# A matrix product with bias and tanh: every engine's order fixed by hand, and an opening in two groups of row tiles and two parts of k

## The chip, the cores and the metric

The kernel runs on one core of one Trainium2 chip. The metric is the device time of one execution in microseconds; a lower time is better. The times shown are three runs of the kernel before, and one further run was executed with the hardware profiler.

## The reference

`a` is 4096 x 4096, `b` is 4096 x 4096, `bias` has 4096 elements, all in fp32. What must be computed:

```python
def reference(a, b, bias):
    return np.tanh(np.matmul(a, b) + bias)
```

## The kernel before

The product is made of matmuls of 128 x 128 weights (a piece of `a`, transposed, in fp16) and a moving operand of 128 x 512 (a piece of `b`, in fp16). There are 32 row tiles of 128 rows of `a`, 32 pieces of k of 128 each, and 8 column halves of 512, so 8192 matmuls. The columns are worked through in 4 chunks of 1024 (`NCW`). For one chunk all of `b`'s 4096 x 1024 piece lies in SBUF in eight tiles `b_0` to `b_7` of four pieces of k each, in two buffers: the next chunk is loaded while this one is worked on.

All loads are issued by POOL and convert fp32 to fp16 on the way. A tile is loaded by four DMAs, one for each quarter of the partitions (32 partitions each), because k is split over the partitions as four quarters of 1024. `load_b` (L55) loads 256 KB (in fp16) a DMA, `load_a` (L62) a quarter of the natural tile `an`. VectorE (DVE) then turns each 32 x 32 block of `an` into the tile `at` (`transpose_a`, L69), which is what the matmuls read as weights. When a PSUM bank has its 32 pieces of k, `finish` adds the bias on DVE (L90, `o_sb<-ps,bias_bc`), takes tanh on ScalarE (ACT, L96), and stores 256 KB from the SyncE queue (L99). `o_sb` has four buffers, `an` two, `at` four, PSUM eight banks.

The opening (matmuls of L131) works on four row tiles at once (`M0`), in eight slices of four pieces of k: it loads 128 KB of `a` four times and 256 KB of `b` four times for a slice, turns `a`, and lets 32 matmuls run into eight banks. After the eighth slice the eight banks are finished. The main loop (matmuls of L166) then goes through the other row tiles of chunk 0 and all row tiles of chunks 1 to 3, each with two banks of 32 matmuls. `load_row_tile` loads and turns the row tile two ahead, and two DMAs of the next chunk's `b` are issued with each row tile until its 32 are done.

The order in which each engine gets its instructions is not that of the text: Tile's scheduler plans it when the program is built. The program's text says what depends on what; the scheduler decides, for instance, whether DVE gets the turning of a later row tile before or after the bias add of the present one. Each engine then works strictly in the order that it was given.

Of the kernel before, what the change touches and what calls it, by code (L numbers as in the profile page):

```python
# [1 line left out]

# [5 lines left out]

P = 128
Q = 4
QP = 32
NB = 512
fp32 = mybir.dt.float32
fp16 = mybir.dt.float16


@with_exitstack
def kernel(
    ctx: ExitStack,
    tc: tile.TileContext,
    a: bass.AP,
    b: bass.AP,
    bias: bass.AP,
    out: bass.AP,
):  # L30
    nc = tc.nc
    M, K = a.shape
    K2, N = b.shape
    assert (M, K, K2, N) == (4096, 4096, 4096, 4096)

    KQ = K // Q
    KT = K // P
    MT = M // P
    NCW = 1024
    NC = N // NCW  # L40
    J = NCW // NB
    TB = 4
    M0 = 4
    SL = [4] * 8

    bpool = ctx.enter_context(tc.tile_pool(name="bpool", bufs=2))
    anat = ctx.enter_context(tc.tile_pool(name="anat", bufs=2))
    atp = ctx.enter_context(tc.tile_pool(name="atp", bufs=4))
    biasp = ctx.enter_context(tc.tile_pool(name="biasp", bufs=2))
    opool = ctx.enter_context(tc.tile_pool(name="opool", bufs=4))  # L50
    psum = ctx.enter_context(tc.tile_pool(name="psum", bufs=8, space=bass.MemoryType.PSUM))

    def load_b(dst, n0, t0, nt, q):
        src = b[ds(q * KQ + t0 * QP, nt * QP), ds(n0, NCW)]
        nc.gpsimd.dma_start(  # L55
            out=dst[ds(q * QP, QP), :, :],
            in_=src.rearrange("(t p) n -> p t n", p=QP),
        )

    def load_a(dst, m0, nmb, k0, kk, q):  # L60
        src = a[ds(m0, nmb * QP), ds(q * KQ + k0, kk)]
        nc.gpsimd.dma_start(  # L62
            out=dst[ds(q * QP, QP), :, :],
            in_=src.rearrange("(mb p) k -> p mb k", p=QP),
        )

    def transpose_a(at, an, mb0, nmb, nt):

        nc.vector.transpose(  # L69
            at[:, :, ds(mb0 * QP, nmb * QP)].rearrange("P t (mb p) -> P mb t p", p=QP),  # L70
            an[:, ds(mb0, nmb), :].rearrange("P mb (t k) -> P mb t k", k=QP),
        )

    def new_b(n0):
        return [bpool.tile([P, TB, NCW], fp16, name=f"b_{i}") for i in range(KT // TB)]

    def load_bias(n0):
        bias_bc = biasp.tile([P, NCW], fp32, name="bias_bc")
        src = bias[ds(n0, NCW)]
        nc.gpsimd.dma_start(  # L80
            out=bias_bc,
            in_=bass.AP(tensor=src.tensor, offset=src.offset, ap=[[0, P], *src.ap]),
        )
        return bias_bc

    def finish(ps, bias_bc, mi, n0, j, pieces=1):
        w = NB // pieces
        o_sb = opool.tile([P, NB], fp32, name="o_sb")
        for i in range(pieces):
            nc.vector.tensor_tensor(  # L90
                out=o_sb[:, ds(i * w, w)],
                in0=ps[:, ds(i * w, w)],
                in1=bias_bc[:, ds(j * NB + i * w, w)],
                op=mybir.AluOpType.add,
            )
            nc.scalar.activation(  # L96
                o_sb[:, ds(i * w, w)], o_sb[:, ds(i * w, w)], mybir.ActivationFunctionType.Tanh
            )
            nc.sync.dma_start(  # L99
                out=out[ds(mi * P, P), ds(n0 + j * NB + i * w, w)], in_=o_sb[:, ds(i * w, w)]  # L100
            )

    def load_row_tile(mi):
        an = anat.tile([P, Q, KQ], fp16, name="an")
        for q in range(Q):
            load_a(an, mi * P, Q, 0, KQ, q)
        at = atp.tile([P, KT, P], fp16, name="at")
        transpose_a(at, an, 0, Q, KT)
        return at


    b_cur = new_b(0)
    ps0 = [[psum.tile([P, NB], fp32, name="ps") for j in range(J)] for m in range(M0)]
    at0 = []
    t0 = 0
    for s, nt in enumerate(SL):
        an = anat.tile([P, M0 * Q, nt * QP], fp16, name="an")
        at = atp.tile([P, nt, M0 * P], fp16, name="at0", bufs=3)
        for q in range(Q):
            load_a(an, 0, M0 * Q, t0 * QP, nt * QP, q)  # L120
        for q in range(Q):
            load_b(b_cur[s], 0, t0, nt, q)
        for m in range(M0):
            transpose_a(at, an, m * Q, Q, nt)
        order = (
            [(t, m, j) for t in range(nt) for m in range(M0) for j in range(J)]
            if s < len(SL) - 1
            else [(t, m, j) for m in range(M0) for j in range(J) for t in range(nt)]
        )
        for t, m, j in order:  # L130
            nc.tensor.matmul(  # L131
                ps0[m][j],
                at[:, t, ts(m, P)],
                b_cur[s][:, t, ts(j, NB)],
                start=t0 + t == 0,
                stop=t0 + t == KT - 1,
            )
        t0 += nt

    bias_bc = load_bias(0)  # L140
    at_q = [load_row_tile(M0), load_row_tile(M0 + 1)]
    for m in range(M0):
        for j in range(J):
            finish(ps0[m][j], bias_bc, m, 0, j)


    todo = [(c, mi) for c in range(NC) for mi in range(MT) if (c, mi) >= (0, M0)]
    b_next, left = None, []
    for i, (c, mi) in enumerate(todo):
        if mi == 0:  # L150
            b_cur, bias_bc = b_next, bias_next
        if c + 1 < NC and mi == (M0 if c == 0 else 0):
            b_next = new_b(c + 1)
            left = [(s, q) for s in range(KT // TB) for q in range(Q)]
        if i + 2 < len(todo):
            at_q.append(load_row_tile(todo[i + 2][1]))
        for s, q in left[:2]:
            load_b(b_next[s], (c + 1) * NCW, s * TB, TB, q)
        left = left[2:]
        if c + 1 < NC and mi == MT - 4:  # L160
            bias_next = load_bias((c + 1) * NCW)
        at = at_q.pop(0)
        for j in range(J):
            ps = psum.tile([P, NB], fp32, name="ps")
            for t in range(KT):
                nc.tensor.matmul(  # L166
                    ps,
                    at[:, t, :],
                    b_cur[t // TB][:, t % TB, ts(j, NB)],
                    start=t == 0,  # L170
                    stop=t == KT - 1,
                )
            last = i == len(todo) - 1 and j == J - 1
            finish(ps, bias_bc, mi, c * NCW, j, pieces=4 if last else 1)


# [1 line left out]
_INS = ['a', 'b', 'bias']  # L178
_OUTS = [((4096, 4096), 'float32')]


# [23 lines left out]
```

## Time and profile before

| what | value |
|---|---|
| median of three runs | 1944.84 us (1944.42 to 1945.73) |
| the profiled execution's own time | 1943.61 us |
| its span, first to last instruction | 1941.8 us |
| mean granted TensorE clock | 0.973 of full |
| PE busy | 1812.3 us (93%), 8192 matmuls |
| DVE busy | 736.3 us (38%), 415 instructions |
| ACT busy | 162.6 us (8%) |
| POOL busy | 357.5 us (18%), 664 instructions |
| DMA over the span | 238.27 MB counted as fp16 or fp32 where it lands, mean 123 GB/s |

Busy time of an engine is the time in which it executes; what stands between busy stretches is waiting. The span is PE's busy time, the waits of PE, the time before its first matmul and the time after its last. A matmul of 512 columns at half clock takes twice as long and counts as busy, so a loss of clock hides in the busy time. In the rows, times are microseconds from the start of the span; a row that ends in `[5.19 <-DVE at L69]` says that the engine stood idle for 5.19 us before this work and that a DVE instruction of line 69, which writes `at`, ended the wait.

### The profile page before, as it was taken

The numbers are of one execution on the slowest core, as the hardware profiler recorded it, in microseconds if no ns is written. First come the engines' busy times: TensorE is split into PE (matmuls) and PEld (weight loads), VectorE is DVE, ScalarE is ACT, GpSimd is POOL, SyncE is SP. The second block draws the span as 40 slices with busy tenths as digits, with TensorE's granted clock in tenths as the row PEclk, the third lists the DMA queues.
The fourth block names the chain that finished last, engine by engine and source line by source line (L and its number), as shares of the span: only waits on it lengthen the run. The fifth ranks groups of instructions, "written<-read, shape, count | busy, mean of one in ns | idle before, by whom it ended". The sixth has DMA issues, their size and how long they took to land. (4 is left out here: it accounts for less than half of the span.)

```text
span 1941.8 us, 19313 instructions
## 1 busy us (share of the span) xinstructions
PE 1812.3 (93%) x8192; PEld 809.6 (42%) x8192; DVE 736.3 (38%) x415; ACT 162.6 (8%) x260; POOL 357.5 (18%) x664
## 2 busy tenths in 40 slices
PE   6698878799999888799999988889999999999998
PEld 2243333344444333344444433334444444444444
DVE  2433233344433333444443333334444444343431
ACT  0100000000000000000000000000000000000000
POOL 5411111011211111111121112111111111111100
PEclk9899989999999999899999999989999999999999
DMA  9976656466675566356667656556666655555531
GB/s 179 201 146 130 130 110 124 98 120 135 126 156 114 120 125 130 80 119 126 136 123 155 135 111 127 119 104 117 125 134 125 125 111 117 112 116 115 114 82 38
DMA packets 144710, 238.27 MB, mean 123 GB/s; under 512 B 31088, under 2 KB 31600, under 8 KB 144624
## 3 DMA queue, kind: packets, MB, share of 16 engines
q0 software_dynamic: 107328, 169.91, 52.4%
q1 hardware_dynamic: 37296, 67.13, 9.4%
q8 instruction: 64, 1.05, 0.2%
q14 instruction: 22, 0.18, 0.0%
HBM read 337.64 MB, written 67.11 MB: 208 GB/s over the span
## 5 line engine op out<-in xcount | busy, mean ns | idle before, releaser
L166 PE MATMUL ps<-b,at 128*128 128x512 f16 x7936 | 1753.2, 385 | 106.3 <-DVE at L69 106.3
L166 PEld LDWEIGHTS <-at 128*128 128x128 f16 x7936 | 784.3, 99 | 1075.1 <-DVE at L69 115.6
L90 DVE TENSOR_TENSOR o_sb<-ps,bias_bc 128x512 f32<-128x512 f32 (+1 forms) x259 | 177.0, 685 | 1154.0 <-PE ps L166 808.2
L69 DVE STREAM_TRANSPOSE at<-an 128x4096 f16<-128x4096 f16 (+1 forms) x156 | 569.3, 3663 | 47.5 <-DMA an<-in_a_dram 47.5
L62 POOL DMA_DIRECT2D an<-in_a_dram x528 | 286.4, 549 | 1455.0 <-DVE at L69 1433.5
L96 ACT ACTIVATE o_sb<-o_sb 128x512 f32<-128x512 f32 (+1 forms) x259 | 161.4, 624 | 1774.8 <-DVE o_sb L90 1774.8
L55 POOL DMA_DIRECT2D b<-in_b_dram x128 | 69.1, 544 | 48.6 <-PE ps L166 23.3
L131 PE MATMUL ps<-b,at 128*128 128x512 f16 x256 | 59.1, 392 | 18.3 <-DMA b<-in_b_dram 18.3
L131 PEld LDWEIGHTS <-at 128*128 128x128 f16 x256 | 25.3, 100 | 51.6 <-issue 24.5
L80 POOL DMA_DIRECT2D bias_bc<-in_bias_dram x4 | 2.2, 560 | 0.2 <-issue 0.2
L96 ACT ACT_TABLE_LOAD x1 | 1.3, 1283 | 0.7 <-PEq L189 0.7
L189 POOL MEMSET const-float32-0.0<- 128x1 f32 x1 | 0.1, 98 | 0.2 <-issue 0.2
L189 POOL MEMSET const-bfloat16-1.0<- 128x1 bf16 x1 | 0.1, 102 | 0.0
L189 POOL MEMSET const-float32-1.0<- 128x1 f32 x1 | 0.1, 98 | 0.0
L189 POOL MEMSET const-uint8-127<- 128x1 uint8 x1 | 0.1, 98 | 0.0
## 6 DMA issues: line engine op xcount, KB each, us to landing
an<-in_a_dram POOLq DMA_DIRECT2D x496, 256.0 KB, 5.3
out_dram<-o_sb SPq DMA_DIRECT2D x255, 256.0 KB, 2.3
b<-in_b_dram POOLq DMA_DIRECT2D x128, 256.0 KB, 7.9
an<-in_a_dram POOLq DMA_DIRECT2D x32, 128.0 KB, 7.5
bias_bc<-in_bias_dram POOLq DMA_DIRECT2D x4, 512.0 KB, 8.1
out_dram<-o_sb SPq DMA_DIRECT2D x4, 64.0 KB, 1.6
```

The source lines that it names most:

```text
L55: nc.gpsimd.dma_start(out=dst[ds(q * QP, QP), :, :], in_=src.rearrange("(t p) n -> p t n", p=QP),)
L62: nc.gpsimd.dma_start(out=dst[ds(q * QP, QP), :, :], in_=src.rearrange("(mb p) k -> p mb k", p=QP),)
L69: nc.vector.transpose(at[:, :, ds(mb0 * QP, nmb * QP)].rearrange("P t (mb p) -> P mb t p", p=QP), an[:, ds(mb0, nmb), :].rearrange("P mb ( ...
L80: nc.gpsimd.dma_start(out=bias_bc, in_=bass.AP(tensor=src.tensor, offset=src.offset, ap=[[0, P], *src.ap]),)
L90: nc.vector.tensor_tensor(out=o_sb[:, ds(i * w, w)], in0=ps[:, ds(i * w, w)], in1=bias_bc[:, ds(j * NB + i * w, w)], op=mybir.AluOpType.add,)
L96: nc.scalar.activation(o_sb[:, ds(i * w, w)], o_sb[:, ds(i * w, w)], mybir.ActivationFunctionType.Tanh)
L131: nc.tensor.matmul(ps0[m][j], at[:, t, ts(m, P)], b_cur[s][:, t, ts(j, NB)], start=t0 + t == 0, stop=t0 + t == KT - 1,)
L166: nc.tensor.matmul(ps, at[:, t, :], b_cur[t // TB][:, t % TB, ts(j, NB)], start=t == 0, stop=t == KT - 1,)
L189: nc = _bacc.Bacc("TRN2", target_bir_lowering=False, num_devices=1)
```

## The change

Tile's scheduler is switched off with `tc.manual_schedule()`: each engine gets its instructions in the order of the program's text. The main loop is written so that the load of a row tile stands three row tiles ahead (`ahead = 3`, with three `an` buffers), and its turning (`new_at`) two ahead, at the start of an iteration, before the matmuls and the bias adds of that iteration.

The opening works on eight row tiles instead of four, in two groups of four (`G`), and on k in two parts: the first eight pieces (`KS`), then the other 24. First part: group 0 goes through slices of 2, 2 and 4 pieces (`S0`), all eight banks at once, then group 1 (row tiles 4 to 7) does its eight pieces bank by bank. Each bank's sum of the first part gets the bias added and is put aside in SBUF in fp32 (`put_aside`, 16 adds of 128 x 512). Second part: group 0 goes through six slices of four pieces (`S2`), and `end` adds the sum put aside in place of the bias, followed by tanh and store; then group 1 does its 24 pieces bank by bank with its own `turn` of 128 x 3072 for each row tile. The sums put aside and group 1's `at` tiles lie in the second buffers of `b_0` to `b_7`, which chunk 1 needs only later. Group 1's first part is loaded by two loads of two row tiles each (four DMAs of 128 KB each), its second part by four loads of a row tile each (four DMAs of 192 KB each).

The diff (`...` stands for the removed lines of the old opening, which the kernel above shows):

```diff
--- before.py
+++ after.py
@@ -40,39 +40,49 @@
     NC = N // NCW
     J = NCW // NB
     TB = 4
-    M0 = 4
-    SL = [4] * 8
+    G = 4
+    KS = 8
+    S0 = [2, 2, 4]
+    S2 = [4] * 6
 
     bpool = ctx.enter_context(tc.tile_pool(name="bpool", bufs=2))
-    anat = ctx.enter_context(tc.tile_pool(name="anat", bufs=2))
+    anat = ctx.enter_context(tc.tile_pool(name="anat", bufs=3))
     atp = ctx.enter_context(tc.tile_pool(name="atp", bufs=4))
     biasp = ctx.enter_context(tc.tile_pool(name="biasp", bufs=2))
     opool = ctx.enter_context(tc.tile_pool(name="opool", bufs=4))
     psum = ctx.enter_context(tc.tile_pool(name="psum", bufs=8, space=bass.MemoryType.PSUM))
-    def load_b(dst, n0, t0, nt, q):
+    ctx.enter_context(tc.manual_schedule())
+
+    def new_b():
+        return [
+            bpool.tile([P, TB, NCW], fp16, name=f"b_{i}", tag=f"b_{i}") for i in range(KT // TB)
+        ]
+
+    def load_b(bt, n0, t0, nt, q):
         src = b[ds(q * KQ + t0 * QP, nt * QP), ds(n0, NCW)]
         nc.gpsimd.dma_start(
-            out=dst[ds(q * QP, QP), :, :],
+            out=bt[t0 // TB][ds(q * QP, QP), ds(t0 % TB, nt), :],
             in_=src.rearrange("(t p) n -> p t n", p=QP),
         )
 
-    def load_a(dst, m0, nmb, k0, kk, q):
-        src = a[ds(m0, nmb * QP), ds(q * KQ + k0, kk)]
-        nc.gpsimd.dma_start(
-            out=dst[ds(q * QP, QP), :, :],
-            in_=src.rearrange("(mb p) k -> p mb k", p=QP),
-        )
-    def transpose_a(at, an, mb0, nmb, nt):
+    def load_a(m0, nmb, t0, nt):
+        an = anat.tile([P, nmb, nt * QP], fp16, name="an")
+        for q in range(Q):
+            src = a[ds(m0, nmb * QP), ds(q * KQ + t0 * QP, nt * QP)]
+            nc.gpsimd.dma_start(
+                out=an[ds(q * QP, QP), :, :],
+                in_=src.rearrange("(mb p) k -> p mb k", p=QP),
+            )
+        return an
+
+    def transpose_a(at, an, mb0, t0, nt):
 
         nc.vector.transpose(
-            at[:, :, ds(mb0 * QP, nmb * QP)].rearrange("P t (mb p) -> P mb t p", p=QP),
-            an[:, ds(mb0, nmb), :].rearrange("P mb (t k) -> P mb t k", k=QP),
-        )
-    def new_b(n0):
-        return [bpool.tile([P, TB, NCW], fp16, name=f"b_{i}") for i in range(KT // TB)]
+            at[:, ds(t0, nt), :].rearrange("P t (mb p) -> P mb t p", p=QP),
+            an[:, ds(mb0, Q), :].rearrange("P mb (t k) -> P mb t k", k=QP),
+        )
 
     def load_bias(n0):
         bias_bc = biasp.tile([P, NCW], fp32, name="bias_bc")
@@ -83,14 +93,19 @@
         )
         return bias_bc
 
-    def finish(ps, bias_bc, mi, n0, j, pieces=1):
+    def mm(ps, at, bt, t, j, start, stop):
+        nc.tensor.matmul(
+            ps, at[:, t, :], bt[t // TB][:, t % TB, ts(j, NB)], start=start, stop=stop
+        )
+
+    def finish(ps, addend, mi, n0, j, pieces=1):
         w = NB // pieces
         o_sb = opool.tile([P, NB], fp32, name="o_sb")
         for i in range(pieces):
             nc.vector.tensor_tensor(
                 out=o_sb[:, ds(i * w, w)],
                 in0=ps[:, ds(i * w, w)],
-                in1=bias_bc[:, ds(j * NB + i * w, w)],
+                in1=addend[:, ds(i * w, w)],
                 op=mybir.AluOpType.add,
             )
             nc.scalar.activation(
@@ -100,78 +115,139 @@
                 out=out[ds(mi * P, P), ds(n0 + j * NB + i * w, w)], in_=o_sb[:, ds(i * w, w)]
             )
 
-    def load_row_tile(mi):
-        an = anat.tile([P, Q, KQ], fp16, name="an")
-        for q in range(Q):
-            load_a(an, mi * P, Q, 0, KQ, q)
+
+    b_cur = new_b()
+    spill = [
+        bpool.tile([P, 4, NB], fp32, name=f"spill_{i}", tag=f"b_{i}") for i in range(2 * G * J // 4)
+    ]
+    ats = [atp.tile([P, KT, P], fp16, name="at") for m in range(G)] + [
+        bpool.tile([P, KT, P], fp16, name=f"atx_{m}", tag=f"b_{4 + m}") for m in range(G)
+    ]
+
+    def aside(m, j):
+        return spill[(m * J + j) // 4][:, (m * J + j) % 4, :]
+
+    def put_aside(ps, m, j):
+        nc.vector.tensor_tensor(
+            out=aside(m, j), in0=ps, in1=bias_bc[:, ts(j, NB)], op=mybir.AluOpType.add
+        )
+
+    def end(ps, m, j):
+        finish(ps, aside(m, j), m, 0, j)
+
+    def banks():
+        return [[psum.tile([P, NB], fp32, name="ps") for j in range(J)] for m in range(G)]
+
+    def group0(slices, t0, t1, done):
+        ps = None
+        first = t0
+        for nt in slices:
+            an = load_a(0, G * Q, t0, nt)
+            for q in range(Q):
+                load_b(b_cur, 0, t0, nt, q)
+            for m in range(G):
+                transpose_a(ats[m], an, m * Q, t0, nt)
+            if t0 == first and first > 0:
+                yield
+            ps = ps or banks()
+            if t0 + nt < t1:
+                for t in range(t0, t0 + nt):
+                    for m in range(G):
+                        for j in range(J):
+                            mm(ps[m][j], ats[m], b_cur, t, j, t == first, False)
+            else:
+                yield
+                for m in range(G):
+                    for j in range(J):
+                        for t in range(t0, t0 + nt):
+                            mm(ps[m][j], ats[m], b_cur, t, j, t == first, t == t1 - 1)
+                        done(ps[m][j], m, j)
+            t0 += nt
+
+    def group1(t0, t1, done, before):
+        for m in range(G, 2 * G):
+            for j in range(J):
+                before(m, j)
+                ps = psum.tile([P, NB], fp32, name="ps")
+                for t in range(t0, t1):
+                    mm(ps, ats[m], b_cur, t, j, t == t0, t == t1 - 1)
+                done(ps, m, j)
+
+
+    g0 = group0(S0, 0, KS, put_aside)
+    next(g0)
+    bias_bc = load_bias(0)
+    an1 = [load_a((G + 2 * h) * P, 2 * Q, 0, KS) for h in range(2)]
+    for _ in g0:
+        pass
+    for m in range(G):
+        transpose_a(ats[G + m], an1[m // 2], (m % 2) * Q, 0, KS)
+
+
+    g0 = group0(S2, KS, KT, end)
+
+    def start_group0(m, j):
+        if (m, j) == (2 * G - 1, 0):
+            next(g0)
+
+    group1(0, KS, put_aside, start_group0)
+
+
+    next(g0)
+    an1 = [load_a((G + m) * P, Q, KS, KT - KS) for m in range(G)]
+    for _ in g0:
+        pass
+
+
+    ahead = 3
+    todo = [(c, mi) for c in range(NC) for mi in range(MT) if (c, mi) >= (0, 2 * G)]
+    an_q = [load_a(mi * P, Q, 0, KT) for c, mi in todo[:ahead]]
+    at_q = []
+
+    def new_at():
         at = atp.tile([P, KT, P], fp16, name="at")
-        transpose_a(at, an, 0, Q, KT)
+        transpose_a(at, an_q.pop(0), 0, 0, KT)
         return at
 
...
+    def turn(m):
+        transpose_a(ats[G + m], an1[m], 0, KS, KT - KS)
+
+    def turn_next(m, j):
+        if j == 0 and m < 2 * G - 1:
+            turn(m + 1 - G)
+        elif m == 2 * G - 1:
+            at_q.append(new_at())
+
+    turn(0)
+    group1(KS, KT, end, turn_next)
+
     b_next, left = None, []
     for i, (c, mi) in enumerate(todo):
         if mi == 0:
             b_cur, bias_bc = b_next, bias_next
-        if c + 1 < NC and mi == (M0 if c == 0 else 0):
-            b_next = new_b(c + 1)
+        if c + 1 < NC and mi == (2 * G if c == 0 else 0):
+            b_next = new_b()
             left = [(s, q) for s in range(KT // TB) for q in range(Q)]
-        if i + 2 < len(todo):
-            at_q.append(load_row_tile(todo[i + 2][1]))
+        if i + ahead < len(todo):
+            an_q.append(load_a(todo[i + ahead][1] * P, Q, 0, KT))
         for s, q in left[:2]:
-            load_b(b_next[s], (c + 1) * NCW, s * TB, TB, q)
+            load_b(b_next, (c + 1) * NCW, s * TB, TB, q)
         left = left[2:]
         if c + 1 < NC and mi == MT - 4:
             bias_next = load_bias((c + 1) * NCW)
+        if an_q and i + 2 < len(todo):
+            at_q.append(new_at())
         at = at_q.pop(0)
         for j in range(J):
             ps = psum.tile([P, NB], fp32, name="ps")
             for t in range(KT):
-                nc.tensor.matmul(
-                    ps,
-                    at[:, t, :],
-                    b_cur[t // TB][:, t % TB, ts(j, NB)],
-                    start=t == 0,
-                    stop=t == KT - 1,
-                )
+                mm(ps, at, b_cur, t, j, t == 0, t == KT - 1)
             last = i == len(todo) - 1 and j == J - 1
-            finish(ps, bias_bc, mi, c * NCW, j, pieces=4 if last else 1)
+            finish(ps, bias_bc[:, ts(j, NB)], mi, c * NCW, j, pieces=4 if last else 1)
 
 
 # ---- launch: one core; inputs and outputs as the reference has them ----
```

## Rows read from the trace of the kernel before

**Rows 1.** The waits, longest first: us in total, times, longest.

```profile
PE ps L166 <- DVE at L69: 106.3, 19, 12.4
...
POOL b L55 <- PE ps L166: 23.3, 2, 14.3
...
PE ps L131 <- DMA b<-in_b_dram: 18.3, 6, 13.6
```

**Rows 2.** Timeline of PE, whole span: start, length, count, idle before and its releaser.

```profile
13.58 23.80 PE L131 MATMUL ps<-b,at 128*128 128x512 f16 x96 [13.58 <-DMA b<-in_b_dram]
38.19 7.07 PE L131 MATMUL ps<-b,at 128*128 128x512 f16 x32 [0.81 <-DMA b<-in_b_dram]
46.14 7.07 PE L131 MATMUL ps<-b,at 128*128 128x512 f16 x32 [0.89 <-DMA b<-in_b_dram]
...
70.33 7.07 PE L131 MATMUL ps<-b,at 128*128 128x512 f16 x32 [1.21 <-DMA b<-in_b_dram]
89.79 85.42 PE L166 MATMUL ps<-b,at 128*128 128x512 f16 x384 [12.40 <-DVE at L69]
180.40 29.25 PE L166 MATMUL ps<-b,at 128*128 128x512 f16 x128 [5.19 <-DVE at L69]
...
1299.67 637.18 PE L166 MATMUL ps<-b,at 128*128 128x512 f16 x2944 [5.19 <-DVE at L69]
```

**Rows 3.** Timeline of DVE just before the pause that ends at 180.40 us.

```profile
175.31 0.69 DVE L90 TENSOR_TENSOR o_sb<-ps,bias_bc 128x512 f32<-128x512 f32 x1 [6.21 <-PE ps L166]
175.91 4.43 DVE L69 STREAM_TRANSPOSE at<-an 128x4096 f16<-128x4096 f16 x1
```

**Rows 4.** Timeline of DVE in a stretch without pauses: adds one row tile apart.

```profile
599.41 0.69 DVE L90 TENSOR_TENSOR o_sb<-ps,bias_bc 128x512 f32<-128x512 f32 x1 [6.21 <-PE ps L166]
...
613.22 0.69 DVE L90 TENSOR_TENSOR o_sb<-ps,bias_bc 128x512 f32<-128x512 f32 x1 [6.21 <-PE ps L166]
```

**Rows 5.** Windows: us, busy time (count) of each engine, granted clock, DMA share, GB/s.

```profile
20.00:80.00 60.00, 52.71 (x241) 22.97 (x239) 17.59 (x29) 2.42 (x4) 29.68 (x51) 1.00 1.32 206
...
181.00:184.00 3.00, 3.00 (x10) 1.06 (x8) 0.00 (x0) 0.00 (x0) 2.85 (x6) 0.61 0.69 98
...
1300.00:1936.00 636.00, 636.00 (x2941) 288.06 (x2940) 258.31 (x136) 57.30 (x91) 94.75 (x177) 1.00 0.55 112
```

**Rows 6.** Timeline of the opening: POOL's loads, DVE, and the weight loads' change of pace.

```profile
1.30 2.68 POOL L62 DMA_DIRECT2D an<-in_a_dram  x4 [0.85 <-POOLq L189]
...
8.56 2.49 DVE L69 STREAM_TRANSPOSE at<-an 128x512 f16<-128x512 f16 x4 [8.56 <-DMA an<-in_a_dram]
...
19.51 17.38 PEld L131 LDWEIGHTS <-at 128*128 128x128 f16 x81 [0.28 <-issue]
...
62.90 0.56 POOL L80 DMA_DIRECT2D bias_bc<-in_bias_dram  x1 [0.16 <-issue]
...
72.32 2.48 DVE L90 TENSOR_TENSOR o_sb<-ps,bias_bc 128x512 f32<-128x512 f32 x4 [4.86 <-PE ps L131]
...
79.84 0.69 DVE L90 TENSOR_TENSOR o_sb<-ps,bias_bc 128x512 f32<-128x512 f32 x1 [5.04 <-DMA out_dram<-o_sb]
...
84.69 0.69 DVE L90 TENSOR_TENSOR o_sb<-ps,bias_bc 128x512 f32<-128x512 f32 x1 [0.41 <-DMA out_dram<-o_sb]
```

**Rows 7.** Groups of instructions by form: busy us, mean ns, idle before.

```profile
L69 DVE STREAM_TRANSPOSE at<-an 128x4096 f16<-128x4096 f16 x124 | 549.4, 4433 | 0.0
...
L90 DVE TENSOR_TENSOR o_sb<-ps,bias_bc 128x512 f32<-128x512 f32 x255 | 176.1, 692 | 1147.8 <-PE ps L166 802.0 <-issue 333.1 <-DMA out_dram<-o_sb 7.1
...
L69 DVE STREAM_TRANSPOSE at<-an 128x512 f16<-128x512 f16 x32 | 19.9, 680 | 47.5 <-DMA an<-in_a_dram 47.5
```

**Rows 8.** The page's DMA issues: size of one, median us from issue to landing.

```profile
an<-in_a_dram POOLq DMA_DIRECT2D x496, 256.0 KB, 5.3
out_dram<-o_sb SPq DMA_DIRECT2D x255, 256.0 KB, 2.3
```

**Rows 9.** Loads of `an` in the first 90 us: issue to landing.

```profile
DMA to landing us min/median/max: 3.1/7.6/11.7
```

More of the change, by code (lines that the diff above doesn't have):

```diff
@@ L51 @@
     psum = ctx.enter_context(tc.tile_pool(name="psum", bufs=8, space=bass.MemoryType.PSUM))
-    def load_b(dst, n0, t0, nt, q):
+    ctx.enter_context(tc.manual_schedule())
[4 more added lines that the diff above has]
+    def load_b(bt, n0, t0, nt, q):
         src = b[ds(q * KQ + t0 * QP, nt * QP), ds(n0, NCW)]
         nc.gpsimd.dma_start(
-            out=dst[ds(q * QP, QP), :, :],
+            out=bt[t0 // TB][ds(q * QP, QP), ds(t0 % TB, nt), :],
             in_=src.rearrange("(t p) n -> p t n", p=QP),
         )
-    def load_a(dst, m0, nmb, k0, kk, q):
-        src = a[ds(m0, nmb * QP), ds(q * KQ + k0, kk)]
-        nc.gpsimd.dma_start(
-            out=dst[ds(q * QP, QP), :, :],
-            in_=src.rearrange("(mb p) k -> p mb k", p=QP),
-        )
-    def transpose_a(at, an, mb0, nmb, nt):
-        nc.vector.transpose(
-            at[:, :, ds(mb0 * QP, nmb * QP)].rearrange("P t (mb p) -> P mb t p", p=QP),
-            an[:, ds(mb0, nmb), :].rearrange("P mb (t k) -> P mb t k", k=QP),
-        )
-    def new_b(n0):
-        return [bpool.tile([P, TB, NCW], fp16, name=f"b_{i}") for i in range(KT // TB)]
+    def load_a(m0, nmb, t0, nt):
[8 more added lines that the diff above has]
+    def transpose_a(at, an, mb0, t0, nt):
+        nc.vector.transpose(
+            at[:, ds(t0, nt), :].rearrange("P t (mb p) -> P mb t p", p=QP),
+            an[:, ds(mb0, Q), :].rearrange("P mb (t k) -> P mb t k", k=QP),
+        )
     def load_bias(n0):
@@ L107, in load_row_tile @@
+    at_q = []
+    def new_at():
         at = atp.tile([P, KT, P], fp16, name="at")
-        transpose_a(at, an, 0, Q, KT)
+        transpose_a(at, an_q.pop(0), 0, 0, KT)
         return at
[L112 to L128, printed above, removed]
-        )
-        for t, m, j in order:
-            nc.tensor.matmul(
[L132 to L136, printed above, removed]
-            )
-        t0 += nt
@@ L140 @@
[L140 to L147, printed above, removed]
+    def turn(m):
[5 more added lines that the diff above has]
+            at_q.append(new_at())
@@ L165 @@
             for t in range(KT):
-                nc.tensor.matmul(
-                    ps,
-                    at[:, t, :],
-                    b_cur[t // TB][:, t % TB, ts(j, NB)],
-                    start=t == 0,
-                    stop=t == KT - 1,
-                )
+                mm(ps, at, b_cur, t, j, t == 0, t == KT - 1)
             last = i == len(todo) - 1 and j == J - 1
-            finish(ps, bias_bc, mi, c * NCW, j, pieces=4 if last else 1)
+            finish(ps, bias_bc[:, ts(j, NB)], mi, c * NCW, j, pieces=4 if last else 1)
 _INS = ['a', 'b', 'bias']
```

## The prediction, made before the changed kernel ran

> **What bounds the kernel now.** I read the list of waits first. PE, the engine that does all the multiplying, loses 106.3 us in 19 waits for DVE's turning of a row tile (the longest is 12.4) and 18.3 us in six waits for loads of b, which include the 13.58 before its first matmul [rows 1]. The timeline of PE alone then shows where: an opening of 256 matmuls to 77.4, the pause of 12.40, and from 180 to 1300 eighteen pauses of about 5.19 us, in runs of seven, six and five that are some 34 us apart, with none for hundreds of microseconds between the runs; the last 2944 matmuls run without one [rows 2]. DVE's own timeline tells what such a pause is: the add at 175.31 waits for the bank that PE has just filled, the turning of 4.43 us stands behind it, and PE starts at 180.40, when that is done [rows 3]. The row tile turned is the one PE needs next; DVE was idle for 6.21 us before the add. So this is order and not load. The adds of a row tile in a stretch without pauses are 13.81 us apart (613.22 - 599.41) [rows 4], which makes 128 row tiles of 64 matmuls 1768 us of PE at full clock.
>
> The windows give the rest: after a pause the granted clock is 0.61 of full for 3 us (1.2 GHz for most of it), while the 60 us of the opening with its gaps of 0.8 to 1.2 us, and the 636 us without pauses, stand at 1.00, that is 2.4 GHz [rows 2, 5]. 128 matmuls after a pause take 29.25 us and not 27.6, so 1.6 are lost there.
>
> The span adds up: 13.58 before the first matmul, 4.7 in the opening's small gaps (18.3 - 13.58), 106.3 in waits for DVE, 1812.3 busy, and 1941.8 - 1936.85 = 4.95 after the last, 1941.8 in all [rows 1, 2]. The busy time holds 1768 of matmuls at full clock, 3.1 at the start (96 matmuls in 23.80 for 20.7), about 2.5 after the 12.40 pause (384 in 85.42 for 82.9), under 1 of rounding in the row ends, and thus some 38 after the 18 pauses, 2.1 each.
>
> **The change part by part: the main loop.** The turning of row tile i+2 now stands on DVE at the start of iteration i, behind the last add of row tile i-1 and ahead of the two adds of row tile i. That add ends about 0.8 us after PE begins row tile i; 4.43 of turning follow [rows 7], done at 5.2; PE needs the tile at 27.6. The add of row tile i's first bank is due at 6.9, so it doesn't wait either. The tile's natural copy was issued when its buffer came free, which is when row tile i-1 had been turned, 41.4 - 5.2 = 36.2 us before it is asked for; loads of this size land in 5.3 us (median), 11.7 at worst in the crowded opening [rows 8, 9]. `at` has four buffers and the one taken belongs to row tile i-2, which PE has left. On POOL the two loads of b behind it can wait for PE at the start of a chunk, which cost 14.3 us of POOL before [rows 1]; 36.2 covers that with the landing time. Chunk 1's b goes into the buffers that held sums and group 1's tiles; its 32 loads begin with row tile 8, two a row tile, so they end 8 row tiles before they are needed, and I cost that at nothing (without that cover POOL would wait for the last of group 1's adds, as it did 14.3 us in the row above). ACT and SP have the same instructions in the same sequence. I therefore take all eighteen pauses as gone: 106.3 - 12.4 = 93.9, and 38 of clock.
>
> **The opening.** First matmul. DVE could begin at 8.56 when four loads of 128 KB of a had landed, and PE at 13.58 when four of 256 KB of b had: 1.25 each [rows 2, 6]. A slice of the opening takes 7.95 (46.14 - 38.19), so its four of a take 7.95 - 5.0 = 2.95, 0.74 each. With slices of two pieces b halves, which saves 2.5. The loads of a halve in bytes but keep their 512 runs a DMA, now 128 B long. Bounds: 0.74 each as before (first matmul at 11.1), half of it (9.6). I take the middle at the upper side, 10.6, since 128 KB in short runs already costs 0.74 where 1.25 / 2 = 0.63 would be its share by bytes. At half clock the weight loads change pace at 19.51, 5.9 us after the start [rows 6]: 14 matmuls at 0.43, so the first 16 end at 10.6 + 6.4 = 17.0, the next 16 at 20.4. The eight pieces are all there at 13.58 + 7.95 = 21.5 by bytes, and 2.95 later if short runs cost the same as before; I take 22.8. PE waits 2.4, and the 32 matmuls end at 29.8.
>
> The Trainium skill speaks against these short pieces: "DMA: Bandwidth & Descriptors", section Bandwidth, asks for DMAs of 1 MiB or more and lists 64 KB at 0.95 us. By that the eight loads would end 7.6 - 2.95 = 4.7 us later than by bytes, an estimate from the page, and the sum below would be 3.4 higher. The row of this case has 128 KB at 0.74 with others in flight, which disagrees with such a price, and I keep the row.
>
> First pause between groups. DVE has the eight `put_aside` adds (0.69 each, PE ends a bank every 0.86, so they keep up) and behind them group 1's turnings of 128 x 1024. From 680 ns for 512 columns and 4433 for 4096 these are about 1.15 [rows 7]. As in the pauses of before, 0.1 + 0.6 + 1.15 + 0.06 = 1.9 us of PE [rows 3]. Group 1's 64 matmuls then take 13.8, to 45.5, and its turnings stay ahead (1.15 against 3.45 a row tile). The 16 `put_aside` adds are 11 us of DVE beside PE's work. The six slices take 41.4, to 86.9.
>
> Do loads keep up there? After 22.8 come the bias (512 KB, twice 1.25), eight of 128 KB (5.9), then a slice each 7.95: the sixth lands at 78.9, and PE begins it at 45.5 + 34.5 = 80.0. The buffers of `an` come free in time: the fourth slice takes the one turned in front of the last row tile of group 1, at about 45, and would be issued at 47. The margin is 1 us, so late loads cost what exceeds it. The second part is turned behind the last slice's eight adds.
>
> Second pause between groups. `turn(0)` has 128 x 3072, about 3.35, and stands behind the eighth `end`. Without more that is 0.1 + 0.6 + 3.35 + 0.06 = 4.1. But the fifth add needs an `o_sb` whose store has landed. Before, the first add began at 72.32 and the eighth at 84.69, 12.4 later, the fifth 5.04 late for a store, while nine loads of 256 to 512 KB issued from 62.90 on were still moving [rows 6]. Now the first add comes 6.0 ahead of the bank that is last, so the same store times would make the eighth 6.3 late: a pause of 10.3. The loads that compete are twelve of 192 KB, from which some 4 us have passed when the stores begin, about 1.4 MB against 2.1 left before. I take two thirds, 4.0, so 8.1 us, and 2.1 for the clock behind it. Ends: 4.1 and 10.3, clock 1.5 to 3. Of the two short waits (2.4 and 1.9) I take no loss of clock, since the nearest gap seen, 1.21, had none [rows 2, 5]; up to 2.1 each if they do.
>
> **The sum.** 1768.3 of matmuls + 10.6 + 3.1 of clock at the start + 2.4 + 1.9 + 8.1 + 2.1 + 0.5 of row ends + 4.95 behind the last matmul = 1802.0. The profiled execution took 1943.61 for a span of 1941.8, so 1803.8; the shown median is 1.2 above that execution, so 1805. Of the 139 us gained 132 are the main loop's.
>
> **The rivals.**
> *Transfers bind in the opening.* Short runs at 0.74 or more, and each later slice late since the margin is 1 us, perhaps a third short pause with loss of clock: 1.7 + 2 + 4, so 1813. For it speaks the margin; against it that every delay of the first part shifts PE's need as well.
> *The order does not come out as I read it.* If DVE still gets the turnings behind adds as before, the eighteen pauses stay and only the opening's 7 us are gained: 1937. Half of them: 1871. Against it: in the text nothing stands between the turning and the iteration before.
> *Slower.* A load that lands late now blocks DVE, with the adds in order behind it, and so the banks and PE, in each row tile. Three buffers make three row tiles a turn of landing + 4.5 us. It begins to bind at a landing of 37 us (3 x 13.81 - 4.5) and makes the kernel slower than before where the row tile loses over 139 / 120 = 1.16 us, at a landing of 40.4. At 42 it would take 1805 + 120 x 1.7 = 2009. The longest landing seen is 11.7 [rows 9].
>
> **How the numbers follow.** The forecast has 0.78, transfers that bind 0.14, pauses that stay 0.05, slower 0.02, no change that can be told (within 0.2%, about 4 us, which is what a measurement of this kernel can tell from none) 0.01. The forecast's own range goes from 1797 (first matmul 1 earlier, second pause 4.1, no wait for the third slice) to 1812 (pause of 10.3, clock lost at the short waits). With the case of late transfers the range is 1796 to 1818.
>
> **What would show it.** PE's timeline: no wait for DVE at the turning after about 100 us; first matmul near 10.6; waits of about 2 near 20 and 30; one of 4 to 10 near 87, with adds waiting for stores. The list of waits: under 15 us for DVE in all, and the granted clock at 1.00 from 100 on. Wrong would be pauses every few row tiles, or slices of the second part that begin after a wait for b.

## The result and the profile after

The changed kernel takes 1808.66 us (median of four runs, 1804.91 to 1809.87) against 1944.72: a ratio of 0.9296, 95% interval 0.928 to 0.9312. Its profiled execution took 1804.91 us with a span of 1803.1; it is the fastest of the four.

PE's timeline, whole span, answers to [rows 2] (start, length, line, count, idle before and its releaser):

```profile
10.91 9.18 PE L97 MATMUL ps<-b,at 128*128 128x512 f16 x32 [10.91 <-DMA b<-in_b_dram]
24.03 7.07 PE L97 MATMUL ps<-b,at 128*128 128x512 f16 x32 [3.95 <-DMA b<-in_b_dram]
33.03 13.99 PE L97 MATMUL ps<-b,atx 128*128 128x512 f16 x64 [1.94 <-DVE atx L82]
46.86 41.60 PE L97 MATMUL ps<-b,at 128*128 128x512 f16 x192
97.38 43.16 PE L97 MATMUL ps<-b,atx 128*128 128x512 f16 x192 [8.92 <-DVE atx L82]
140.38 1657.76 PE L97 MATMUL ps<-b,at 128*128 128x512 f16 x7680
```

The eighteen pauses of [rows 2] are gone: the loop's 7680 matmuls stand in one row, without a wait. The opening does 512 matmuls with three waits. The six slices of the second part run as one row of 192, so no load was late there; `atx` is group 1's `at`.

The list of waits, answering to [rows 1]:

```profile
PE ps L97 <- DMA b<-in_b_dram: 14.9, 2, 10.9
...
PE ps L97 <- DVE atx L82: 10.9, 2, 8.9
```

PE waits for DVE 10.9 us in two places, in place of 106.3 in 19. The span adds up again: 25.7 of waits (10.91 of them before the first matmul), 1772.4 busy, 4.96 after the last matmul.

DVE's timeline in the loop, to set beside [rows 3]:

```profile
154.45 0.69 DVE L105 TENSOR_TENSOR o_sb<-ps,bias_bc 128x512 f32<-128x512 f32 x1 [6.21 <-PE ps L97]
155.06 4.43 DVE L82 STREAM_TRANSPOSE at<-an 128x4096 f16<-128x4096 f16 x1
```

The turning still stands right behind an add that waited for PE. What differs is whose turning it is: here it is for the row tile after next, which PE asks for some 22 us after 155.06 + 4.43; in [rows 3] it was for the very next.

The windows, as in [rows 5]: the clock is 1.00 in the loop, and 0.50 just behind the pause of 8.92.

```profile
97.00:100.00 3.00, 2.62 (x7) 0.97 (x8) 3.00 (x2) 0.00 (x0) 2.14 (x4) 0.50 0.39 36
...
140.00:1798.00 1658.00, 1658.00 (x7683) 751.52 (x7681) 679.92 (x359) 151.15 (x240) 300.53 (x562) 1.00 0.64 129
```

### The profile page after: what moved, and what is told of

The parts are those of the page before. It is cut to its first block, busy times and chain, and to the rows that moved or that the text cites. A ratio compares the mean times of both kernels' runs of the same rounds, so it can differ in the third digit from the quotient of the medians.

```text
span 1803.1 us, 19295 instructions
## 1 busy us (share of the span) xinstructions
PE 1772.4 (98%) x8192; PEld 802.1 (44%) x8192; DVE 747.5 (41%) x439; ACT 162.8 (9%) x260; POOL 366.5 (20%) x680
## 4 chain that ended last, share of the span: by engine, by line
PE 94%; ACT 0%; DVE 0%; ACTq 0%; issue 0%; DVEq 0%
PE ps L97 94%; ACT o_sb L111 0%; DVE o_sb L105 0%; ACTq L276 0%; DVEq L105 0%
## 5 line engine op out<-in xcount | busy, mean ns | idle before, releaser
L97 PE MATMUL ps<-b,at 128*128 128x512 f16 x7936 | 1715.6, 379 | 14.9 <-DMA b<-in_b_dram 14.9
L97 PEld LDWEIGHTS <-at 128*128 128x128 f16 x7936 | 776.9, 98 | 952.8 <-issue 18.1
L105 DVE TENSOR_TENSOR o_sb<-ps,bias_bc 128x512 f32<-128x512 f32 (+1 forms) x243 | 166.2, 685 | 978.2 <-PE ps L97 763.8
L82 DVE STREAM_TRANSPOSE at<-an 128x4096 f16<-128x4096 f16 (+2 forms) x156 | 552.4, 3554 | 32.1 <-DMA an<-in_a_dram 32.1
L74 POOL DMA_DIRECT2D an<-in_a_dram x540 | 293.5, 550 | 1312.1 <-DVE at L82 1246.2
L97 PE MATMUL ps<-b,atx 128*128 128x512 f16 x256 | 57.1, 386 | 10.9 <-DVE atx L82 10.9
L97 PEld LDWEIGHTS <-atx 128*128 128x128 f16 x256 | 25.3, 99 | 42.7 <-DVE atx L82 11.8
L105 DVE TENSOR_TENSOR o_sb<-ps,spill 128x512 f32<-128x512 f32 x16 | 11.0, 692 | 31.9 <-PE ps L97 19.9
L82 DVE STREAM_TRANSPOSE atx<-an 128x1024 f16<-128x1024 f16 (+1 forms) x8 | 18.0, 2285 | 0.0
L133 DVE TENSOR_TENSOR spill<-ps,bias_bc 128x512 f32<-128x512 f32 x16 | 10.7, 684 | 9.3 <-PE ps L97 4.9
```

The costliest lines, as they stand in the source:

```text
L74: nc.gpsimd.dma_start(out=an[ds(q * QP, QP), :, :], in_=src.rearrange("(mb p) k -> p mb k", p=QP),)
L82: nc.vector.transpose(at[:, ds(t0, nt), :].rearrange("P t (mb p) -> P mb t p", p=QP), an[:, ds(mb0, Q), :].rearrange("P mb (t k) -> P mb t ...
L97: nc.tensor.matmul(ps, at[:, t, :], bt[t // TB][:, t % TB, ts(j, NB)], start=start, stop=stop)
L105: nc.vector.tensor_tensor(out=o_sb[:, ds(i * w, w)], in0=ps[:, ds(i * w, w)], in1=addend[:, ds(i * w, w)], op=mybir.AluOpType.add,)
L133: nc.vector.tensor_tensor(out=aside(m, j), in0=ps, in1=bias_bc[:, ts(j, NB)], op=mybir.AluOpType.add)
```

## The experiments

Theory A: the loop's gain comes from the place of the turning in DVE's order, and the opening's remaining waits come from the same kind of place. The rivals: the deeper loading gave the gain (B), the opening carries more of it (C), and those named with the single runs. Medians are of four to ten runs; the kernel before, run beside them, stood at 1944.1 to 1944.9.

**Two buffers of `an`, loads two ahead.**

```diff
-    anat = ctx.enter_context(tc.tile_pool(name="anat", bufs=3))
+    anat = ctx.enter_context(tc.tile_pool(name="anat", bufs=2))
...
-    ahead = 3
+    ahead = 2
```

> The changed kernel with two buffers of an in place of three and row tiles loaded two ahead in place of three. Theory A (the order on DVE gave the loop's gain): no pause of PE in the loop, 1808 us, at most 5 more from an opening in which loads wait for a buffer. Rival B (the deeper loading gave it): turnings are late again, at least the eighteen pauses of before, 1930 us or more.

1811.83 us (ratio 0.9318, 0.9302 to 0.9333). PE's timeline from the second part on:

```profile
57.17 7.07 PE L97 MATMUL ps<-b,at 128*128 128x512 f16 x32 [0.89 <-DMA b<-in_b_dram]
...
103.85 42.98 PE L97 MATMUL ps<-b,atx 128*128 128x512 f16 x192 [7.38 <-DVE atx L82]
146.67 1657.76 PE L97 MATMUL ps<-b,at 128*128 128x512 f16 x7680
```

The loop takes 1657.76 as with three buffers: B falls. The 3 us more are in the opening, where each later slice of the second part now waits 0.9 to 1.1 for b, 4.9 in all; a second pause that is shorter (7.38) gives part of that back.

**Late turnings, order by hand.** At 18 places of the loop, six row tiles apart, the turning that PE needs next goes behind the last add.

```diff
-        if an_q and i + 2 < len(todo):
+        late = i % 6 == 4 and i < 108
+        held = late or (i % 6 == 3 and i < 108)
+        if an_q and i + 2 < len(todo) and not held:
             at_q.append(new_at())
...
             finish(ps, bias_bc[:, ts(j, NB)], mi, c * NCW, j, pieces=4 if last else 1)
+        if late:
+            at_q += [new_at(), new_at()]
```

> The changed kernel, in which at 18 places of the loop, six row tiles apart, the turning of the next row tile is put behind the last bias add of the present one, as the scheduler had done in the kernel before. Loads, buffers and opening stay. Theory A: 18 pauses of PE of 5.2 us each, 93 us in all, and 2.1 us of lost clock behind each, so about 131 us more: 1940 us. Rival B (loading three ahead covers it): within 5 us of the changed kernel's 1808.

1944.73 us (ratio 0.9998, 0.9989 to 1.0007): the whole gain is undone. A wait and two rows of PE:

```profile
PE ps L97 <- DVE at L82: 93.5, 18, 5.2
```

```profile
217.82 85.58 PE L97 MATMUL ps<-b,at 128*128 128x512 f16 x384 [5.20 <-DVE at L82]
308.59 84.58 PE L97 MATMUL ps<-b,at 128*128 128x512 f16 x384 [5.20 <-DVE at L82]
```

Each pause is the 5.2 of [rows 3], and 384 matmuls behind it take 84.6 to 85.8 in place of 82.9, so 1.7 to 2.9 of clock, 2.3 on average. 93.5 and 18 times 2.3 make 135 of the 136 us between this run and 1808.66; the expectation had 2.1 of clock a pause. Place alone, with the loads, buffers and opening of the changed kernel, costs as much as the whole change had gained.

**The scheduler's order with the new text.**

```diff
-    ctx.enter_context(tc.manual_schedule())
```

> The changed kernel with the scheduler's order instead of the order by hand; text, loads three ahead, three buffers and the opening in two groups stay. Theory A: the scheduler again puts turnings behind adds that wait for PE, pauses of 5.2 us come back, 1900 to 1940 us if as many as before. Rival B (the rewritten loop and its buffers are enough): 1808 to 1815 us.

1945.09 us (ratio 1.0002, 0.9992 to 1.0011): no change against the kernel before, although the opening and the loop's text are the new ones. A wait, rows of PE, and DVE ahead of the first of the pauses:

```profile
PE ps L96 <- DVE at L81: 98.7, 19, 5.2
```

```profile
99.34 43.33 PE L96 MATMUL ps<-b,atx 128*128 128x512 f16 x192 [8.47 <-DVE atx L81]
142.50 83.04 PE L96 MATMUL ps<-b,at 128*128 128x512 f16 x384
230.74 30.36 PE L96 MATMUL ps<-b,at 128*128 128x512 f16 x128 [5.19 <-DVE at L81]
```

```profile
225.64 0.69 DVE L104 TENSOR_TENSOR o_sb<-ps,bias_bc 128x512 f32<-128x512 f32 x1 [6.22 <-PE ps L96]
226.25 4.43 DVE L81 STREAM_TRANSPOSE at<-an 128x4096 f16<-128x4096 f16 x1
```

Nineteen pauses, in runs as before. The order is that of [rows 3]: the turning stands behind an add that waited for PE, and PE goes on at 230.74, when it is done. The 512th matmul ends at 142.5; before it ended at about 147.6 (89.79 + 85.42 less the 27.6 of the last 128 of that row [rows 2]). So the new opening gains 5, and one pause more takes 5.2 and some clock back.

**The old opening with the new loop.** Order by hand; one group of four row tiles, eight slices, all eight banks finished before `at_q += [new_at(), new_at()]`.

```diff
-    todo = [(c, mi) for c in range(NC) for mi in range(MT) if (c, mi) >= (0, 2 * G)]
+    todo = [(c, mi) for c in range(NC) for mi in range(MT) if (c, mi) >= (0, M0)]
...
-    turn(0)
-    group1(KS, KT, end, turn_next)
+    for m in range(M0):
+        for j in range(J):
+            finish(ps0[m][j], bias_bc[:, ts(j, NB)], m, 0, j)
+    at_q += [new_at(), new_at()]
```

> The order by hand and the new loop behind the old opening (one group of four row tiles, eight slices of four pieces of k, the eight banks finished before the first turning of a whole row tile). Theory A: the loop alone gives 132 us of the gain and the opening 7, so 1815 us, with a first matmul near 13.6 and one pause of 10 to 13 us near 77. Rival C (the two groups carry a larger part, because the loop needs the later start): 1830 us or more.

1813.63 us (ratio 0.9325, 0.9311 to 0.9339). PE, first and last row:

```profile
13.62 23.18 PE L97 MATMUL ps<-b,at 128*128 128x512 f16 x96 [13.62 <-DMA b<-in_b_dram]
...
91.01 1715.88 PE L97 MATMUL ps<-b,at 128*128 128x512 f16 x7936 [13.41 <-DVE at L82]
```

The loop alone gives 131 us (1944.9 - 1813.6), the opening 5 (against 1808.66) to 7 (against the 1807.02 of the next run). Theory A had 132 and 7; C falls.

**The changed kernel again,** as the base for the next runs, without an edit.

> The changed kernel again, as the base for the three runs beside it. 1808.7 us, single runs between 1805 and 1810; if the spread comes from the clock behind the wait of about 4 us for the third slice (0 or 1.7 us) and behind the pause of 8.9 (1.7 to 3), the spans differ by up to some 4 us while the waits in the profile stay the same.

1807.02 us (1806.57 to 1807.58; ratio 0.9293, 0.9281 to 0.9306). One row of PE:

```profile
23.98 8.75 PE L97 MATMUL ps<-b,at 128*128 128x512 f16 x32 [4.16 <-DMA b<-in_b_dram]
```

Behind the wait for the third slice 32 matmuls take 8.75 here, 7.07 in the first profile. The granted clock shows it: 0.50 of full (1.2 GHz) from 26 to 28 us here, 1.00 (2.4 GHz) in the first profile. This makes 1.7 of the 2.7 us between the two spans (1805.8 and 1803.1); the second pause, 9.52 and not 8.92, and 0.4 more of clock behind it are the rest. The waits differ little, as expected, and the clock behind them is 2.1 of the 2.7 between these two executions.

**Two slices of four in the first part.**

```diff
-    S0 = [2, 2, 4]
+    S0 = [4, 4]
```

> The changed kernel whose first part has two slices of four pieces of k in place of 2, 2 and 4. Theory A (a DMA of a with 512 short runs costs POOL 0.64 us to issue and the queue little less than one twice as long, so short slices start PE early and make it wait later): first matmul at 13.6 in place of 10.9, no wait of 4 us behind it, first part done at 30.5 in place of 31.1, and no clock lost there: 1806 to 1808 us, 0.6 to 3 faster than the changed kernel. Rival D (the earlier start is kept to the end of the part): 2.7 us slower, 1811.

1805.38 us (1803.38 to 1807.1; ratio 0.9286, 0.9274 to 0.9299). The interval overlaps the base's, so the time alone doesn't settle a gain of 1.6; that it is not slower does speak against D. PE:

```profile
14.23 15.92 PE L97 MATMUL ps<-b,at 128*128 128x512 f16 x64 [14.23 <-DMA b<-in_b_dram]
32.09 13.99 PE L97 MATMUL ps<-b,atx 128*128 128x512 f16 x64 [1.94 <-DVE atx L82]
```

PE begins 3.3 later (2.7 was expected) and still ends the part at 30.15, before the 31.1 of the changed kernel: the early start is lost in the wait for the third slice. POOL's timeline of the changed kernel, then of this one, shows the other half:

```profile
6.05 2.56 POOL L74 DMA_DIRECT2D an<-in_a_dram  x4
8.60 1.11 POOL L65 DMA_DIRECT2D b<-in_b_dram  x2
...
11.57 2.55 POOL L74 DMA_DIRECT2D an<-in_a_dram  x4
14.11 2.24 POOL L65 DMA_DIRECT2D b<-in_b_dram  x4
```

```profile
6.13 2.62 POOL L74 DMA_DIRECT2D an<-in_a_dram  x4
10.63 0.55 POOL L65 DMA_DIRECT2D b<-in_b_dram  x1 [1.88 <-DMA b<-in_b_dram]
```

Four loads of a cost POOL 2.55 whether they carry 64 KB each (6.05) or 128 (11.57). With short slices POOL issues almost without rest to 16.3; with long ones it waits for landings from 8.75 on. The loads of the second slice then land 4.1 to 5.1 us after their issue in the changed kernel and 7.7 to 9.0 here, where they are twice as large. This points to the issue, and not the queue alone, as what holds the short slices back; no run changes the issue by itself.

**Seven buffers of `o_sb`.**

```diff
-    opool = ctx.enter_context(tc.tile_pool(name="opool", bufs=4))
+    opool = ctx.enter_context(tc.tile_pool(name="opool", bufs=7))
```

> The changed kernel with seven buffers of o_sb in place of four, so that of the eight adds behind group 0 only the last waits for a store (the first). Theory A (the second pause of 8.9 us is 4.1 of order and 4.8 of waiting for stores): the pause becomes 4.1 to 6, 1804 to 1806 us. Rival E (the pause is the late landing of what is turned): pause and time unchanged.

1804.34 us (1803.62 to 1804.88; ratio 0.9279, 0.9267 to 0.9292); no run of the base is that fast, though the two intervals overlap a little. DVE, then PE:

```profile
92.39 0.69 DVE L105 TENSOR_TENSOR o_sb<-ps,spill 128x512 f32<-128x512 f32 x1 [1.40 <-DMA out_dram<-o_sb]
93.00 6.63 DVE L82 STREAM_TRANSPOSE atx<-an 128x3072 f16<-128x3072 f16 x2
```

```profile
96.42 43.26 PE L97 MATMUL ps<-b,atx 128*128 128x512 f16 x192 [5.29 <-DVE atx L82]
```

Only the eighth add waits for a store, 1.40 us, and the pause falls from 9.52 to 5.29: E falls. The 4.2 are not all that the stores cost, since a wait for one is left. DVE of the changed kernel, first profile:

```profile
92.72 1.32 DVE L105 TENSOR_TENSOR o_sb<-ps,spill 128x512 f32<-128x512 f32 x2 [0.60 <-DMA out_dram<-o_sb]
93.96 6.63 DVE L82 STREAM_TRANSPOSE atx<-an 128x3072 f16<-128x3072 f16 x2
```

The eighth add ends at 94.04 there. PE had left its bank at 88.46 (46.86 + 41.60), so without stores it would have ended at about 89.2. Of the pause of 8.92 that makes 4.8 of stores and 4.1 of order; of the base's 9.52 it is 5.4 if the order costs the same.

**The first turning ahead of group 0's last adds.**

```diff
     an1 = [load_a((G + m) * P, Q, KS, KT - KS) for m in range(G)]
+    transpose_a(ats[G], an1[0], 0, KS, KT - KS)
     for _ in g0:
         pass
...
-    turn(0)
     group1(KS, KT, end, turn_next)
```

> The changed kernel with the first turning of group 1's second part ahead of group 0's eight last adds on DVE, in place of behind them. Theory A (the order on DVE makes the second pause): the pause of 8.9 us goes with 1.7 of clock behind it, 1798 us, 10.6 faster. Rival F (the adds that are now later hand the wait on to the banks that group 1 needs): a wait for a bank of 4 us or more takes its place, 1803 us or more.

1802.53 us (ratio 0.927, 0.9257 to 0.9283): 4.5 faster, not 10.6. PE, then DVE:

```profile
90.93 10.52 PE L97 MATMUL ps<-b,atx 128*128 128x512 f16 x48
104.42 32.66 PE L97 MATMUL ps<-b,atx 128*128 128x512 f16 x144 [2.97 <-DVE atx L82]
```

```profile
97.32 0.69 DVE L105 TENSOR_TENSOR o_sb<-ps,spill 128x512 f32<-128x512 f32 x1 [6.04 <-DMA out_dram<-o_sb]
98.93 2.15 DVE L105 TENSOR_TENSOR o_sb<-ps,spill 128x512 f32<-128x512 f32 x3 [0.92 <-DMA out_dram<-o_sb]
101.00 3.37 DVE L82 STREAM_TRANSPOSE atx<-an 128x3072 f16<-128x3072 f16 x1
```

The long pause went and a shorter one came a row tile later: the second turning now stands behind the adds that wait for stores. It is no wait for a bank, so F is not it; A was right in kind, but I had not followed the order one turning further.

**The second turning between the fourth and the fifth last add,** beside the edit above.

```diff
-    g0 = group0(S2, KS, KT, end)
+    def end_group0(ps, m, j):
+        end(ps, m, j)
+        if (m, j) == (1, 1):
+            transpose_a(ats[G + 1], an1[1], 0, KS, KT - KS)
+
+    g0 = group0(S2, KS, KT, end_group0)
...
-        if j == 0 and m < 2 * G - 1:
+        if j == 0 and G < m < 2 * G - 1:
```

> The kernel of the run that turned first, with the second turning of group 1 put on DVE between group 0's fourth and fifth last add, ahead of the adds that wait for stores. Theory A (the 3 us pause left there, one row tile later, stood behind the adds that wait for stores): it goes with 1.5 us of clock, so 1798 us, 9 faster than the changed kernel's 1807.0 beside the last runs. Rival F (banks, not the turning, hold PE): the pause stays, 1802.5.

1796.37 us (ratio 0.9239, 0.9226 to 0.9251), 10.7 below the base. PE:

```profile
48.52 41.60 PE L97 MATMUL ps<-b,at 128*128 128x512 f16 x192
89.96 41.60 PE L97 MATMUL ps<-b,atx 128*128 128x512 f16 x192
131.40 1657.76 PE L97 MATMUL ps<-b,at 128*128 128x512 f16 x7680
```

From 48.5 to the end PE doesn't wait. The adds still wait for stores, and nothing that PE needs is behind them.

**Group 1's first two turnings of the first part ahead of the adds that put group 0's sums aside.**

```diff
+    for m in range(2):
+        transpose_a(ats[G + m], an1[0], m * Q, 0, KS)
     for _ in g0:
         pass
-    for m in range(G):
-        transpose_a(ats[G + m], an1[m // 2], (m % 2) * Q, 0, KS)
+    for m in range(2, G):
+        transpose_a(ats[G + m], an1[1], (m - 2) * Q, 0, KS)
```

> The changed kernel with group 1's first two turnings of the first part ahead of the eight adds that put group 0's sums aside. Theory A (the first pause of 1.94 us is those adds ahead of the turning): the pause goes, 1805.0 us against 1807.0. Rival F (the adds are late instead and PE waits for a bank): a wait for an add of 1 to 3 us in its place, 1806 to 1808.

1805.65 us (ratio 0.9287, 0.9274 to 0.93), an interval that overlaps the base's. The profile has the pause gone and no wait for a bank in its place; this execution lost more clock behind the wait for the third slice (9.85 for the 32 matmuls), which hides a part of the gain:

```profile
24.82 9.85 PE L97 MATMUL ps<-b,at 128*128 128x512 f16 x32 [3.77 <-DMA b<-in_b_dram]
34.50 13.98 PE L97 MATMUL ps<-b,atx 128*128 128x512 f16 x64
```

**All together:** two slices of four, and the last three edits of order.

> All that helped or should help together: two slices of four pieces of k in the first part, both pauses' turnings ahead of the adds. 1807.0 - 9 - 1.9 - 1.6 gives 1794.5 us. If the gains overlap (the loads then come too late for the slices of the second part, whose margin was 1 us by the prediction and is eaten by every gain ahead of it): waits for b of up to 1 us a slice, 1797 to 1799.

1792.65 us (1792.1 to 1793.23; ratio 0.922, 0.9207 to 0.9232), 16 below the changed kernel's 1808.66 and 14 below the base's 1807.02. PE:

```profile
14.61 15.42 PE L97 MATMUL ps<-b,at 128*128 128x512 f16 x64 [14.61 <-DMA b<-in_b_dram]
30.25 13.97 PE L97 MATMUL ps<-b,atx 128*128 128x512 f16 x64 [0.21 <-DVE spill L133]
44.06 41.78 PE L97 MATMUL ps<-b,at 128*128 128x512 f16 x192
86.66 41.60 PE L97 MATMUL ps<-b,atx 128*128 128x512 f16 x192 [0.83 <-DVE o_sb L105]
```

Behind the first matmul 1.0 us of waits is left, and no wait for b in the second part: the gains don't overlap (1807.0 less the single 10.7, 1.4 and 1.6 makes 1793.3). The 0.83 is a wait for a bank, the kind that F had feared, and small. Of the span of 1791.1, 14.6 stand before the first matmul.

## Why the prediction was right, step by step

**The main loop.** Right in place and size: 131 us by the run with the old opening, 132 by the prediction. That order and not loading makes it is shown from both sides: fewer buffers change nothing in the loop, and late turnings with all the rest kept bring the whole loss back. That this text needs the order by hand is shown by the scheduler's run, where the rival "the order does not come out as I read it" is what happens.

**The opening.** First matmul 10.6, measured 10.91. First pause 1.9, measured 1.94 (its turning took 1.21; the two rows that the working names give 1.22, not its 1.15). Second pause 8.1, measured 8.92 and 9.52: the 4.1 of order held, and the stores cost 4.8 and 5.4 where the term had 4.0. Clock behind it 2.1, measured 1.6 and 2.0 (43.16 and 43.58, where 192 matmuls without a wait take 41.60). The second part's loads kept up, by more than the margin of 1: the last load of the sixth slice landed at about 79, as forecast, and PE came to that slice at 81.4.

**The term that was most mis-sized** is the wait for the third slice: 2.4, measured 3.95 (and 4.16 in the second profile). The part's loads were there at 24.0, not 22.8. That is near the later of its two bounds, 24.45, where short runs cost the same as before. The working priced the short loads in the queue alone and left out that POOL needs 0.64 us to issue each load of 512 runs, of 64 KB as of 128 KB; that this is the reason is likely by the run with longer slices, not shown.

**The step that did not hold** is "of the two short waits I take no loss of clock", for the longer of the two. The 1.94 never lost any (13.99 for 64 matmuls in the eight profiles that have it). The wait for the third slice lost none in the first profile (7.07 for 32), but in all eight other profiles that have it, of this kernel and of its variants, where it was 3.77 to 5.21 us long, the 32 matmuls took 8.41 to 9.97, a loss of 1.3 to 2.9. The prediction allowed for this in its range and not in its sum.

**Where luck helped.** The sum for the profiled execution was 1802.0 of span and it had 1803.1, but two errors offset each other in it: the waits were 25.7 where the terms have 23.0, and the lost clock was 3.7 (2.1 at the start, 1.6 behind the second pause) where they have 5.2. This execution was also the fastest of four, and the only profiled one that lost no clock at the third slice. The median is 3.7 us above it, where the working added 1.2. Clock lost at the third slice would explain most of the rest: the other three executions show a mean granted clock of 0.995 to its 0.997, but they have no profile that says where.

On the price by "DMA: Bandwidth & Descriptors" (the Trainium skill, section Bandwidth) the trace stands between: the part came 2.5 us later than by bytes (24.0 against 21.5), where the estimate from the page was 4.7. Its direction is borne out, by the run with longer slices too, as far as that run resolves it.

**The rivals.** Transfers that bind: only in the first part, 1.6 us. Slower by loads that block DVE: no sign, the longest landing of `an` in the whole execution is 12.0 against the 37 from which it would bind, and no turning of the loop waited for a load:

```profile
DMA to landing us min/median/max: 2.7/5.3/12.0
```

## What to carry to other kernels

When PE waits for an engine that is mostly idle, look at what stands ahead of the awaited instruction in that engine's queue, and put work that PE needs ahead of work that waits for PE or for stores. A gain in one stretch can be invisible while a planner places later work anew: here a better opening was worth nothing under the scheduler's order, 5 to 7 us under a fixed one. When a wait is moved, follow the order one step further, since the next instruction behind the same adds may be the next to be late.

## What the runs showed of the hardware

- POOL's issue of a load with 512 runs took 0.64 us with runs of 128 B and of 256 B (fp16) alike (2.56 and 2.55 for four); a load of b with 128 runs of 2 KB took 0.54 (2.15 for four).
- TensorE's clock behind a wait: none lost after 1.94 us in eight profiles; after 3.95 none, after 4.16 in another execution of the same kernel 1.7 us, after 3.77 in the run without the first pause 2.8 (9.85 for 7.07); after 2.97 in the run that turned first about 1.5 (32.66 for 144 matmuls, where 192 without a wait take 41.60). So the length of a wait alone does not tell the loss.
- A store of 256 KB landed 5.8 to 7.0 us after its issue beside loads of 192 KB (issued 83.8 to 86.5 us in the changed kernel), and 2.0 to 2.7 after it when issued from 91 us on, with these loads done or nearly so. The adds ahead of the second pause wait for the late ones.
